# Transformer layers with convolution mixing, one core: a new order string for the mixing stage, three gate products tied behind a layer norm's mean, and a feed-forward whose down products run two blocks behind

## The chip, the cores and the metric

The kernel runs as one program on one core of a Trainium2 chip. The metric is the device time of one execution in microseconds (us). Names of engines: PE is the matrix engine (TensorE), DVE the vector engine, ACT the scalar engine, POOL the general engine (GpSimd), SP the engine that here only issues loads. A "product" below is one matmul instruction.

## The reference, cut to what matters

256 tokens of width 1024 pass through two layers (a gated delta rule layer and a sliding window attention layer, each followed by a gated feed-forward), and then through a third block: mixing (a convolution branch and an attention branch, joined by gates) and an expert layer. The parts that the change touches:

```python
def conv_gated_mlp(hn, w_up, conv_w, conv_b, w_down):      # twice, hidden width 2816
    u = causal_dwconv(hn @ w_up, conv_w, conv_b)           # 3 taps
    gate, val = jnp.split(u, 2, axis=-1)
    return (jax.nn.silu(gate) * val) @ w_down

def conformer_conv(a_in, dw_w, dw_b, ln_g, ln_b, w_pw):    # 1024 channels, 31 taps
    u = a_in[..., :CONV_DIM] * jax.nn.sigmoid(a_in[..., CONV_DIM:])
    u = lax.conv_general_dilated(u, dw_w[:, None, :], ...) + dw_b
    u = layernorm(u, ln_g, ln_b)
    u = jax.nn.silu(u)
    return u @ w_pw

# mixing, z = rmsnorm_2(x) @ w_in
gates = jax.nn.sigmoid(z[..., o_v:]).reshape(b, s, 2, d)
merged = gates[:, :, 0, :] * conv_out + gates[:, :, 1, :] * attn_out
x = x + merged @ w_out
```

## The kernel before

Activations lie transposed: 1024 features are 8 blocks of 128 partitions, and the 256 tokens are the free axis. Every float32 product is made of three products on split operands: `mm3` (L247 to L251) multiplies the weight's high part with the activation's high part (L249) and low part (L250), and the weight's low part with the activation's high part (L251). `wsplit` (L233 to L242) loads 512 KB of a weight (`raw`, issued by SP), rounds it on ACT (`wh`, L242) and subtracts on POOL or DVE (`wl`, L233); a table `LOW` for each stage says on which. `raw`, `wh` and `wl` have four buffers each, so weights run up to four pieces ahead. `proj` is one projection of 256 output columns: 2 weight pieces, 48 products. `kouter` adds 256 hidden features to four accumulators (`pa`): also 48 products.

The stages follow one another: delta rule layer (0 to some 290 us in the trace), feed-forward 0 (to 508), window attention (to 600), feed-forward 1 (to 800), mixing (to some 1075), expert layer (to the end).

**Feed-forward** (`ffn`). A loop over 11 blocks of 256 hidden features. A block makes two projections (gate and value), multiplies them with the norm's factor (L784), runs the three taps (ACT L789, DVE L791), Silu (ACT L794), the product of gate and value (DVE L795), and splits it into `gh` (ACT L798) and `gl` (DVE L799). `lower` then makes the block's down product with `kouter`; it is called for the block before the one just made (`pend`). `residual` adds the accumulators to the stream (DVE L292) and splits the result for the next stage (ACT L373, DVE L374).

**Mixing.** `play` walks through the string `MIX`; each item calls a function: `c0` to `c3` conv_in (two projections for 256 channels), `d0` to `d15` half the taps of one block of 128 channels (`conv`: the first tap on ACT at L1363, 30 multiply-adds on DVE at L1366, on an accumulator that alternates between two for even and odd blocks), `q`, `k`, `S`, `P`, `o` the attention, `g0` to `g7` a gate product (`gate`, L1382: one projection and one DVE multiplication), `L0` center, `N0` norm, `w` the pointwise product of the convolution branch, `e` the output product. `center` sums the convolution's channels with products against ones (`colsum`, L329), forms the mean (DVE L1399), spreads it over partitions (`rowcast`, L309) and subtracts it (DVE L1402). `norm` squares (ACT L315, L318), adds (DVE L319), sums again on PE (L329), takes the power -1/2 (DVE L338, POOL L339), spreads it (L309), multiplies (DVE L1415), applies Silu (ACT L1417) and splits into `upad` (ACT L1420) and `qT` (DVE L1421), the operands of `w0`.

The text order isn't the engines' order: the framework's scheduler reads the program, keeps data dependencies, and writes down a fixed order for each engine. `tc.issue_after(x)` makes it put what follows behind the instruction x. At run time each engine takes its own list strictly in order and waits where an operand is missing.

Of the kernel before, what the change touches and what calls it, by code (L numbers as in the profile page):

```python
# [11 lines left out]
F32R = mybir.dt.float32r  # L12
# [9 lines left out]
P = 128  # L22
T = 256
D = 1024
DB = D // P
# [5 lines left out]
C_SL = 320  # L31
# [7 lines left out]
def shape_constants():  # L39
# [7 lines left out]
    for k in range(DB):  # L47
# [24 lines left out]

GDN = "d0 d1 d2 z0 p0 d3 p1 p2 p3 b0 v1 v0 z1 i0 s1 v2 s0 z2 i2 o1 v3 o0 s2 z3 s3 o2 o3"
SWA = "q2 q0 S0 S1 P0 q1 S3 S2 P1 S4 P3 o0 P2 P4 q3 S5 o1 S7 P7 S6 P5 P6 o2 o3"
MIX = ("c0 q0 d0 d1 q1 d2 c1 d3 k0 d4 S0 S1 d5 P0 q2 d6 P1 S2 c2 d7 S3 P2 d8 q3 P3 d9 S4 c3 d10 S5 P4 d11 g4 S6 d12 "
       "P5 g5 S7 d13 P6 g6 d14 P7 g7 d15 s8 s12 o0 o1 o2 o3 a0 g0 g1 L0 g2 g3 N0 R0 s0 s4 w0 w1 e0 w2 e1 w3 e2 e3")
PEER = " ".join([f"q{i} k{i}" for i in range(8)] + [f"T{i}" for i in range(8)] + [f"u{i}" for i in range(32)])


# [18 lines left out]
class Net:  # L98
# [21 lines left out]
    def t(self, pool, shape, tag, dt=F32, **kw):  # L120
        return pool.tile(shape, dt, tag=tag, name=self.nm(tag), **kw)
# [184 lines left out]


    def rowcast(self, out, col):
        self.nc.tensor.matmul(out, col.to_broadcast([P, P]), self.ident, start=True, stop=True)  # L309

    def tokstat(self, src, pool, tag):

# [446 lines left out]
    def ffn(self, l, nxt, hook=None, each=None):  # L759
        nc, tc, I, t = self.nc, self.tc, self.I, self.t  # L760
        up, down = I["ffn_w_up"][l], I["ffn_w_down"][l]
        cw, cb = self.fconv[l], self.fbias[l]
        self.stage = "ffn"
        x = self.input(self.v["ffn_norm_w"][:, 8 * l : 8 * l + 8])
        with tc.tile_pool(name=f"ffn{l}", bufs=2) as fp:
            _, rrow = self.rstd(self.hT, fp, "sq")
            acc = None
            pend = []
            self.wide, self.nwide = True, NW[0]

            def lower(i, gh, gl):
                nonlocal acc
                if acc is None:
                    acc = self.acc4()
                self.kouter(acc, down, (2 * i, 2 * i + 1), [(gh[:, kk, :], gl[:, kk, :]) for kk in range(2)],
                            i == 0, i == 10)

            for i in range(11):
                if hook:
                    hook(i)  # L780
                cv = []
                for part in range(2):
                    ps = self.proj(up, part * 2816 + 256 * i, x)
                    nc.vector.tensor_mul(ps, ps, self.bc(rrow))  # L784
                    o = t(fp, [P, 2, T], f"cv{part}")
                    for m in range(2):
                        blk = part * 22 + 2 * i + m
                        w = [cw[j][:, blk : blk + 1] for j in range(3)]
                        nc.scalar.activation(o[:, m, :], ps[:, m, :], AF.Identity, scale=w[2], bias=cb[:, blk : blk + 1])  # L789
                        for d in range(1, 3):  # L790
                            nc.vector.scalar_tensor_tensor(o[:, m, d:], ps[:, m, : T - d], w[2 - d], o[:, m, d:],  # L791
                                                           op0=ALU.mult, op1=ALU.add)
                    cv.append(o)
                nc.scalar.activation(cv[0], cv[0], AF.Silu)  # L794
                nc.vector.tensor_mul(cv[0], cv[0], cv[1])  # L795
                gh = t(fp, [P, 2, T], "gh", F32R, bufs=3)
                gl = t(fp, [P, 2, T], "gl", F32R, bufs=3)
                nc.scalar.copy(gh, cv[0])  # L798
                nc.vector.tensor_sub(gl, cv[0], gh.bitcast(F32))  # L799
                pend.append((i, gh, gl))  # L800
                if len(pend) > 1:
                    lower(*pend.pop(0))
            lower(*pend.pop(0))
            self.residual(acc, nxt, None, each)


# [520 lines left out]
    def mix(self):  # L1327
        nc, tc, I, t = self.nc, self.tc, self.I, self.t
        w_in = I["w_in_2"][0]
        wf = self.v["final_norm_w"]  # L1330
        self.stage = "mix"
        x = self.input(self.wfg)
        with tc.tile_pool(name="mix", bufs=1, reuse_waits="tile") as mp, \
# [9 lines left out]
            rrow = self.rrow(rcol)  # L1343
# [10 lines left out]
            qT = t(mp, [P, DB, T], "qT")  # L1354
# [26 lines left out]
            def gate(i):  # L1381
                nc.vector.tensor_mul(gates[:, 2 * i : 2 * i + 2, :], self.proj(w_in, 3584 + 256 * i, x), self.bc(rrow))  # L1382

            def sig(i):
                nc.scalar.activation(gates[:, i : i + 4, :], gates[:, i : i + 4, :], AF.Sigmoid)

# [53 lines left out]
            def resnorm(_):  # L1440

                row = self.rrow(r1, ap, "sc256")
                for k in range(DB):
# [2 lines left out]

            self.wide, self.nwide = True, NW[3]
            self.play(MIX, c=conv_in, d=conv, k=lambda _: self.heads_kv(w_in, 3072, 3328, x, rrow, rcol, kT, v),
                      q=lambda i: self.heads_q(w_in, 2048, x, rrow, qT, i, self.c[:, C_SL : C_SL + DB]), g=gate, s=sig,
                      S=lambda u: self.scores(a, u), P=lambda u: self.values(a, u), o=lambda i: self.out_kv(a, i),  # L1450
                      a=attention, L=center, N=norm, w=point, e=out, R=resnorm)
            self.xq = ExitStack()
# [79 lines left out]
```

## Time and profile before

| | |
|---|---|
| median of 3 runs | 1987.35 us (1985.11 to 1990.6) |
| profiled execution, its own time | 1986.34 us |
| its span in the trace | 1984.6 us |
| mean granted TensorE clock | 0.973 |
| PE busy | 1848.3 us, 93% of the span |
| DVE busy | 1438.0 us, 72% |
| ACT busy | 956.5 us, 48% |
| POOL busy | 671.8 us, 34% |

The profiled execution is 1.0 us faster than the median; what is worked out from its trace is a difference, and is taken off the median too. "Busy" counts an instruction from start to end, and products on PE overlap: one lasts some 0.28 us at full clock, while a new one starts every 0.11 to 0.12 us.

### The profile page before, as it was taken

Reading aid. Unit: us, or ns where it says so; the run is one execution under the profiler, and the core shown is the slowest. Engines: PE = TensorE matmul, PEld = TensorE weight load, DVE = VectorE, ACT = ScalarE, POOL = GpSimd, SP = SyncE. Lnnn points to the kernel's source line nnn. Section 1 sums busy time; section 2 is a strip of 40 time slices with the busy share of each in tenths; the row PEclk is TensorE's granted clock in tenths of the full one; section 3 lists DMA queues with packets and bytes.
Section 4 is the critical chain, followed back from the end, with each engine's and each line's share of the span. In section 5 each row is a group of like instructions: output and inputs, shape, how many; then the busy total and the mean of one; then the engine's idle time right before and its main releaser. Section 6 shows DMA issues by size and latency. Waiting matters only on the chain. (4 is left out here: it accounts for less than half of the span.)

```text
span 1984.6 us, 36930 instructions
## 1 busy us (share of the span) xinstructions
PE 1848.3 (93%) x14537; PEld 1747.2 (88%) x14537; DVE 1438.0 (72%) x2765; ACT 956.5 (48%) x1419; POOL 671.8 (34%) x309
## 2 busy tenths in 40 slices
PE   7979999999899999999968978889999999999998
PEld 7879999999889999989968968779999988887886
DVE  6786656666546666588864799999888878875555
ACT  5744435555656555456444533433333443444443
POOL 4444333444323444655634423334333300000000
PEclk9989999999899999999979999999999999999999
DMA  6454236666424666443524555555555555555665
GB/s 198 118 160 139 86 107 201 191 192 193 134 86 128 212 192 185 135 139 108 170 86 139 161 128 149 140 137 160 155 161 154 149 170 160 163 159 169 195 195 171
DMA packets 243435, 306.29 MB, mean 154 GB/s; under 512 B 26076, under 2 KB 213821, under 8 KB 243133
## 3 DMA queue, kind: packets, MB, share of 16 engines
q1 hardware_dynamic: 240864, 302.84, 50.6%
q8 instruction: 114, 1.87, 0.4%
q10 hardware_dynamic: 2237, 1.07, 0.2%
q14 instruction: 60, 0.49, 0.1%
q0 software_dynamic: 160, 0.02, 0.0%
HBM read 298.60 MB, written 4.74 MB: 153 GB/s over the span
## 5 line engine op out<-in xcount | busy, mean ns | idle before, releaser
L233 POOL TENSOR_TENSOR wl<-raw,wh 128x1024 fp32r<-128x1024 f32 (+1 forms) x196 | 470.5, 2404 | 558.5 <-ACT wh L242 499.8
L242 ACT CAST wh<-raw 128x1024 fp32r<-128x1024 f32 (+1 forms) x285 | 297.8, 1047 | 319.2 <-issue 111.9
L233 DVE TENSOR_TENSOR wl<-raw,wh 128x1024 fp32r<-128x1024 f32 x233 | 294.4, 1264 | 162.2 <-ACT wh L1103 103.4
L251 PE MATMUL pp<-xh,wl 128*128 128x256 f32 x1392 | 394.5, 284 | 16.4 <-DVE wl L1009 16.3
L249 PE MATMUL pp<-xh,wh 128*128 128x256 f32 x1392 | 394.9, 284 | 15.1 <-DVE kq L491 10.3
L251 PE MATMUL pa<-xh,wl 128*128 128x256 f32 (+1 forms) x1336 | 382.0, 286 | 19.7 <-DVE wl L1009 19.6
L249 PE MATMUL pa<-xh,wh 128*128 128x256 f32 (+1 forms) x1336 | 382.9, 287 | 14.4 <-ACT hT L304 6.2
L250 PE MATMUL pp<-xl,wh 128*128 128x256 f32 x1392 | 393.1, 282 | 2.1 <-DVE xl L374 2.1
L250 PE MATMUL pa<-xl,wh 128*128 128x256 f32 (+1 forms) x1336 | 381.1, 285 | 2.0 <-DVE xl L374 1.9
L251 PEld LDWEIGHTS pp<-xh,wl 128*128 128x128 f32 x1392 | 267.0, 192 | 18.8 <-DVE wl L1009 18.3
L249 PEld LDWEIGHTS pp<-xh,wh 128*128 128x128 f32 x1392 | 267.1, 192 | 16.9 <-issue 10.7
L251 PEld LDWEIGHTS pa<-xh,wl 128*128 128x128 f32 (+1 forms) x1336 | 257.3, 193 | 22.4 <-DVE wl L1009 22.4
L249 PEld LDWEIGHTS pa<-xh,wh 128*128 128x128 f32 (+1 forms) x1336 | 257.3, 193 | 16.5 <-ACT hT L304 6.6
L250 PEld LDWEIGHTS pp<-xl,wh 128*128 128x128 f32 x1392 | 266.8, 192 | 2.5 <-DVE xl L374 2.3
L1009 POOL TENSOR_TENSOR wl<-rt,wh 128x1024 fp32r<-128x1024 f32 x64 | 166.0, 2594 | 291.1 <-ACT wh L994 209.2
L250 PEld LDWEIGHTS pa<-xl,wh 128*128 128x128 f32 (+1 forms) x1336 | 257.3, 193 | 3.2 <-DVE xl L374 2.4
L994 ACT CAST wh<-rt 128x1024 fp32r<-128x1024 f32 x128 | 134.3, 1049 | 240.6 <-PE pa L250 104.2
L1103 ACT CAST wh<-raw 128x1024 fp32r<-128x1024 f32 x128 | 135.0, 1055 | 216.4 <-PE pa L1113 210.1
L1112 PE MATMUL pa<-wl,rt 128*128 128x512 f32 x512 | 201.7, 394 | 0.0
L1113 PE MATMUL pa<-wh,rt 128*128 128x512 f32 x512 | 199.5, 391 | 0.0
L1111 PE MATMUL pa<-wh,rt 128*128 128x512 f32 x512 | 164.6, 394 | 1.4 <-ACT rt L1097 1.4
L1154 POOL TENSOR_TENSOR fsb<-fsb,mhalf 128x1 f32<-128x1 f32 x2 | 1.1, 550 | 393.8 <-DVE fsb L1153 393.8
(433 smaller groups left out, 3575.4 us busy)
## 6 DMA issues: line engine op xcount, KB each, us to landing
raw<-in_peer_u_dram SPq DMA_DIRECT2D x512, 128.0 KB
raw<-in_peer_v_dram SPq DMA_DIRECT2D x128, 512.0 KB
raw<-in_ffn_w_up_dram SPq DMA_DIRECT2D x88, 512.0 KB
raw<-in_a_w_in_dram SPq DMA_DIRECT2D x48, 512.0 KB
raw<-in_ffn_w_down_dram SPq DMA_DIRECT2D x44, 512.0 KB
raw<-in_w_in_dram SPq DMA_DIRECT2D x44, 512.0 KB
raw<-in_a_w_out_dram SPq DMA_DIRECT2D x16, 512.0 KB
raw<-in_peer_w_query_dram SPq DMA_DIRECT2D x16, 512.0 KB
```

What stands on the lines that cost most here:

```text
L233: (self.nc.vector if order[self.turn % len(order)] == "D" else self.nc.gpsimd).tensor_tensor(out, raw, high, op=ALU.subtract)
L242: nc.scalar.copy(wh, raw)
L249: mm(out, wh, xh, start=start, stop=False, skip_group_check=skip)
L250: mm(out, wh, xl, start=False, stop=False, skip_group_check=skip)
L251: mm(out, wl, xh, start=False, stop=stop, skip_group_check=skip)
L994: nc.scalar.copy(uh.rearrange("p f (b e) -> p f b e", b=4), rv)
L1009: eng.tensor_tensor(lo.rearrange("p f (b e) -> p f b e", b=4), rv, high.bitcast(F32).rearrange("p f (b e) -> p f b e", b=4), op=ALU.subtract)
L1103: nc.scalar.copy(vh, raw)
L1111: nc.tensor.matmul(o, w2[:, 0, i, s], vh[:, c], start=first, stop=False)
L1112: nc.tensor.matmul(o, w2[:, 0, i, s], vl[:, c], start=False, stop=False)
L1113: nc.tensor.matmul(o, w2[:, 1, i, s], vh[:, c], start=False, stop=last)
L1154: nc.gpsimd.tensor_tensor(o, o, self.mhalf(), op=ALU.pow)
```

## The change

The string MIX gets another order: the convolution's items stand earlier, `g4` to `g7` later. `g1`, `g2` and `g3` become `h1`, `h2` and `h3`, the same products by a function `late`, which puts them behind the last `rowcast` so far: `h1` and `h2` stand behind `L0` (the cast of the mean), `h3` behind `N0`. In the feed-forward `pend` holds two blocks instead of one, `gh` and `gl` get a fourth buffer, and the last two blocks' down products come after the loop.

```diff
-MIX = ("c0 q0 d0 d1 q1 d2 c1 d3 k0 d4 S0 S1 d5 P0 q2 d6 P1 S2 c2 d7 S3 P2 d8 q3 P3 d9 S4 c3 d10 S5 P4 d11 g4 S6 d12 "
-       "P5 g5 S7 d13 P6 g6 d14 P7 g7 d15 s8 s12 o0 o1 o2 o3 a0 g0 g1 L0 g2 g3 N0 R0 s0 s4 w0 w1 e0 w2 e1 w3 e2 e3")
+MIX = ("c0 q0 d0 q1 d1 k0 d2 c1 d3 S0 d4 S1 q2 d5 P0 d6 c2 S2 d7 P1 d8 S3 q3 d9 c3 d10 P2 S4 d11 P3 d12 S5 d13 "
+       "P4 S6 d14 P5 d15 S7 P6 g4 P7 g5 g6 g7 s8 s12 o0 o1 o2 o3 a0 g0 L0 h1 h2 N0 h3 R0 s0 s4 w0 w1 e0 w2 e1 w3 e2 e3")
...
     def rowcast(self, out, col):
-        self.nc.tensor.matmul(out, col.to_broadcast([P, P]), self.ident, start=True, stop=True)
+        self.cast = self.nc.tensor.matmul(out, col.to_broadcast([P, P]), self.ident, start=True, stop=True)
...
-                gh = t(fp, [P, 2, T], "gh", F32R, bufs=3)
-                gl = t(fp, [P, 2, T], "gl", F32R, bufs=3)
+                gh = t(fp, [P, 2, T], "gh", F32R, bufs=4)
+                gl = t(fp, [P, 2, T], "gl", F32R, bufs=4)
                 nc.scalar.copy(gh, cv[0])
                 nc.vector.tensor_sub(gl, cv[0], gh.bitcast(F32))
                 pend.append((i, gh, gl))
-                if len(pend) > 1:
+                if len(pend) > 2:
                     lower(*pend.pop(0))
-            lower(*pend.pop(0))
+            for p in pend:
+                lower(*p)
             self.residual(acc, nxt, None, each)
...
+            def late(i):
+
+                with tc.issue_after(self.cast.ins):
+                    gate(i)
...
-                      q=..., g=gate, s=sig,
+                      q=..., g=gate, h=late, s=sig,
```

What the engines' lists say now is shown at three places. The first is PE at the end of feed-forward 0; `pp` is the last up projection of block 10 (its operand `xh` is the stage's input), `pa` the accumulators, and the number behind `gh` and `gl` names the block's buffer. Before:

```order
L251 MATMUL pp_5697<-xh_3570,wl_5732 128x256
L249 MATMUL pa_3928<-gh_5564,wh_5774 128x256
...
L251 MATMUL pa_3931<-gh_5564,wl_5782 128x256
L249 MATMUL pa_3928<-gh_5768,wh_5834 128x256
L249 MATMUL pa_3929<-gh_5768,wh_5834 128x256
L249 MATMUL pa_3930<-gh_5768,wh_5834 128x256
```

And with the change, at the same place:

```order
L251 MATMUL pp_5637<-xh_3570,wl_5672 128x256
L249 MATMUL pa_4072<-gh_5299,wh_5714 128x256
...
L251 MATMUL pa_4075<-gh_5299,wl_5722 128x256
L249 MATMUL pa_4072<-gh_5504,wh_5774 128x256
...
L251 MATMUL pa_4075<-gh_5504,wl_5782 128x256
L249 MATMUL pa_4072<-gh_5708,wh_5834 128x256
L250 MATMUL pa_4072<-gl_5709,wh_5834 128x256
```

Behind the last up product there stood 48 products on the block before (`gh_5564`) and then those on the last block; now there stand 96 on two earlier blocks ahead of those on the last (`gh_5708`). Feed-forward 1 ends in the same way.

The second place is PE around the layer norm of the mixing stage; `conv` is the convolution's result, `mu` the mean, `sc` the sum of squares, `rcol` and `r` the two factors that are spread, `xh_9260` the mixing stage's input, which marks a gate product, and `upad`, `qT` the operands of `w0`. Before:

```order
L329 MATMUL pm_11498<-ones_85,conv_9332 128x1 x14
L249 MATMUL pa_11521<-xh_9260,wh_11524 128x256
...
L249 MATMUL pp_11583<-xh_9260,wh_11586 128x256
...
L329 MATMUL pm_11498<-ones_85,conv_9332 128x1 x2
L309 MATMUL pm_11516<-c_head_81,mu_11497 128x128 x2
L329 MATMUL pm_11656<-ones_85,sc_1537_11645 128x1 x4
L309 MATMUL pm_11664<-c_head_81,rcol_11661 128x128 x2
L309 MATMUL pm_11693<-c_head_81,r_1241_9314 128x128 x2
L249 MATMUL pp_11714<-upad_11667,wh_11717 128x256
```

With the change:

```order
L329 MATMUL pm_11436<-ones_85,conv_9332 128x1 x16
L309 MATMUL pm_11454<-c_head_81,mu_11435 128x128 x2
L249 MATMUL pa_11459<-xh_9260,wh_11462 128x256
...
L249 MATMUL pa_11521<-xh_9260,wh_11524 128x256
...
L329 MATMUL pm_11594<-ones_85,sc_1530_11583 128x1 x4
L309 MATMUL pm_11602<-c_head_81,rcol_11599 128x128 x2
L309 MATMUL pm_11693<-c_head_81,r_1241_9314 128x128 x2
L249 MATMUL pa_11631<-xh_9260,wh_11634 128x256
...
L249 MATMUL pp_11714<-upad_11605,wh_11717 128x256
```

The gate products `g1` to `g3` (48 products each) stood ahead of the mean's last sum; now `h1` and `h2` stand between the cast of the mean and the sum of squares (`sc`), and `h3` between the last cast and `w0`. `g0` stays ahead.

The third place is DVE's list from the last gate product before the mean on; `pm` at L1366 (L1367 with the change) is the convolution's accumulator. Before:

```order
L1382 TENSOR_TENSOR gates_9342<-pa_11521,rrow_9327 128x512
L1366 SCALAR_TENSOR_TENSOR pm_9333<-upad_9329,colsdw_48_207,pm_9333 128x256 x5
L233 TENSOR_TENSOR wl_11784<-raw_11780,wh_11782 128x1024
L1366 SCALAR_TENSOR_TENSOR pm_9333<-upad_9329,colsdw_48_207,pm_9333 128x256
L1382 TENSOR_TENSOR gates_9342<-pp_11583,rrow_9327 128x512
L1366 SCALAR_TENSOR_TENSOR pm_9333<-upad_9329,colsdw_48_207,pm_9333 128x256 x5
L1366 SCALAR_TENSOR_TENSOR conv_9332<-upad_9329,colsdw_48_207,pm_9333 128x256
L1399 TENSOR_SCALAR mu_11497<-pm_11498 128x2
```

With the change, through to the operands of `w0`:

```order
L1383 TENSOR_TENSOR gates_9342<-pp_11373,rrow_9327 128x512
L1367 SCALAR_TENSOR_TENSOR pm_9333<-upad_9329,colsdw_45_201,pm_9333 128x256 x15
L1367 SCALAR_TENSOR_TENSOR pm_9333<-upad_9329,colsdw_48_207,pm_9333 128x256 x14
L1367 SCALAR_TENSOR_TENSOR conv_9332<-upad_9329,colsdw_48_207,pm_9333 128x256
L1405 TENSOR_SCALAR mu_11435<-pm_11436 128x2
...
L1383 TENSOR_TENSOR gates_9342<-pa_11521,rrow_9327 128x512
L338 TENSOR_SCALAR rcol_11599<-pm_11594 128x2
...
L1427 TENSOR_TENSOR qT_11606<-pp_11607,upad_11605 128x512
L233 TENSOR_TENSOR wl_11784<-raw_11780,wh_11782 128x1024
L1383 TENSOR_TENSOR gates_9342<-pa_11631,rrow_9327 128x512
L1427 TENSOR_TENSOR qT_11606<-pa_11613,upad_11605 128x512
```

Three gate multiplications and two weight low parts have left the stretch ahead of the mean; the multiplications of `h1` and `h2` stand ahead of the norm's `rcol`, and that of `h3` between the first and the second quarter of `qT`. Over the whole stage, 98 of the 240 multiply-adds stood behind the last scores (S7, the last L1208) before, and 120 stand behind them now, while 108 fewer PE rows stand ahead of them.

## Rows read from the trace of the kernel before

**Rows 1.** The page: busy time, share of the span and instructions of each engine.

```profile
PE 1848.3 (93%) x14537; PEld 1747.2 (88%) x14537; DVE 1438.0 (72%) x2765; ACT 956.5 (48%) x1419; POOL 671.8 (34%) x309
```

**Rows 2.** Windows of feed-forward 0: length, busy time and count per engine, PEclk, DMA.

```profile
340.00:360.00 20.00, 20.00 (x174) 20.00 (x173) 14.29 (x19) 10.65 (x15) 8.98 (x4) 1.00 0.69 237
...
500.00:506.00 6.00, 5.71 (x26) 5.71 (x27) 1.54 (x4) 0.47 (x1) 0.00 (x0) 0.50 0.26 87
```

**Rows 3.** Timeline of PE, end of feed-forward 0: start, length, instruction [idle before, releaser].

```profile
490.34 0.28 PE L251 MATMUL pp<-xh,wl 128*128 128x256 f32 x1
...
498.18 0.74 PE L249 MATMUL pa<-gh,wh 128*128 128x256 f32 x4 [1.91 <-ACT gh L798]
500.29 0.58 PE L250 MATMUL pa<-gl,wh 128*128 128x256 f32 x1 [1.38 <-DVE gl L799]
...
508.18 0.28 PE L251 MATMUL pa<-gh,wl 128*128 128x256 f32 x1
```

**Rows 4.** Timelines of DVE, ACT and POOL at the same place.

```profile
498.16 2.08 DVE L799 TENSOR_TENSOR gl<-cv,gh 128x512 fp32r<-128x512 f32 x1 [0.69 <-ACT gh L798]
...
507.25 0.70 DVE L292 TENSOR_TENSOR pa<-pa,hT 128x512 f32<-128x512 f32 x1 [0.77 <-PE pa L251]
507.85 0.87 DVE L374 SCALAR_TENSOR_TENSOR xl<-pa,colsv,xh 128x256 fp32r<-128x256 f32 x2
...
497.51 0.62 ACT L798 CAST gh<-cv 128x512 fp32r<-128x512 f32 x1 [0.28 <-DVE cv L795]
...
497.31 2.38 POOL L233 TENSOR_TENSOR wl<-raw,wh 128x1024 fp32r<-128x1024 f32 x1 [0.38 <-ACT wh L242]
```

**Rows 5.** Line L799 from 330 to 480 us: durations in ns, minimum/median/maximum.

```profile
L799 DVE TENSOR_TENSOR gl<-cv,gh x9: 676/677/691, 339.1 to 465.5; 128x512 fp32r<-128x512 f32 x9
```

**Rows 6.** Timeline of PE, end of feed-forward 1.

```profile
782.63 0.28 PE L251 MATMUL pp<-xh,wl 128*128 128x256 f32 x1
...
790.49 0.74 PE L249 MATMUL pa<-gh,wh 128*128 128x256 f32 x4 [1.85 <-ACT gh L798]
792.64 0.38 PE L250 MATMUL pa<-gl,wh 128*128 128x256 f32 x1 [1.40 <-DVE gl L799]
...
799.38 0.28 PE L251 MATMUL pa<-gh,wl 128*128 128x256 f32 x1
```

**Rows 7.** Windows of the mixing stage: up to the last scores, to the mean, behind it.

```profile
820.00:934.50 114.50, 111.42 (x925) 106.45 (x924) 97.14 (x258) 67.53 (x127) 72.31 (x31) 0.99 0.45 142
934.50:1004.10 69.60, 64.47 (x538) 63.63 (x536) 59.61 (x118) 32.41 (x42) 40.98 (x17) 0.98 0.48 152
...
1006.00:1024.00 18.00, 6.74 (x28) 5.87 (x27) 13.05 (x23) 9.40 (x17) 0.69 (x1) 0.50 0.03 10
```

**Rows 8.** Timeline of DVE: a wait behind the last scores, and the convolution's end.

```profile
938.25 0.16 DVE L1219 TENSOR_TENSOR den<-den,es 128x4 f32<-128x4 f32 x1 [2.05 <-ACT es L1213]
...
998.67 1.23 DVE L233 TENSOR_TENSOR wl<-raw,wh 128x1024 fp32r<-128x1024 f32 x1 [0.55 <-ACT wh L242]
...
1000.38 0.69 DVE L1382 TENSOR_TENSOR gates<-pp,rrow 128x512 f32<-128x512 f32 x1
1000.99 2.58 DVE L1366 SCALAR_TENSOR_TENSOR pm<-upad,colsdw,pm 128x256 f32<-128x256 f32 x5
```

**Rows 9.** Timeline of PE around the mean and ahead of w0.

```profile
1004.14 0.61 PE L329 MATMUL pm<-ones,conv 128*128 128x1 f32 x4 [3.80 <-DVE conv L1366]
1005.00 1.23 PE L309 MATMUL pm<-c_head,mu 128*128 128x128 f32 x4 [0.25 <-DVE mu L1399]
1011.09 1.84 PE L329 MATMUL pm<-ones,sc 128*128 128x1 f32 x8 [4.87 <-DVE sc L319]
1013.96 1.22 PE L309 MATMUL pm<-c_head,rcol 128*128 128x128 f32 x4 [1.03 <-POOL rcol L339]
1014.97 1.06 PE L309 MATMUL pm<-c_head,r 128*128 128x128 f32 x4
...
1021.98 0.58 PE L250 MATMUL pp<-qT,wh 128*128 128x256 f32 x1 [2.38 <-DVE qT L1421]
```

More of the change, by code (lines that the diff above doesn't have):

```diff
@@ L1448, in mix @@
             self.play(MIX, c=conv_in, d=conv, k=lambda _: self.heads_kv(w_in, 3072, 3328, x, rrow, rcol, kT, v),
-                      q=lambda i: self.heads_q(w_in, 2048, x, rrow, qT, i, self.c[:, C_SL : C_SL + DB]), g=gate, s=sig,
+                      q=lambda i: self.heads_q(w_in, 2048, x, rrow, qT, i, self.c[:, C_SL : C_SL + DB]), g=gate, h=late, s=sig,
                       S=lambda u: self.scores(a, u), P=lambda u: self.values(a, u), o=lambda i: self.out_kv(a, i),
```

## The prediction

> **What bounds the kernel now.** I read the busy times first: PE is busy 93% of the span and no other engine comes near [rows 1]. So time can be won in two ways: PE gets less to do, or it waits less and runs less at the low clock. The change removes no product, so only the second is open, and I went through the windows of the stages that it touches for places where PE isn't full.
>
> In the middle of a feed-forward PE is busy 20.00 of 20 us and starts 174 to 176 products in that time, one every 0.114 us, at granted clock 1.00 [rows 2]; an order changed inside it can win nothing. The end is different. The timeline shows two waits on the last block: 1.91 us for `gh` and 1.38 us for `gl`, and then products at clock 0.50, half of the full 2.4 GHz: 26 recorded in 5.71 us [rows 2, 3]. Feed-forward 1 ends alike, with 1.85 and 1.40 us [rows 6].
>
> In the mixing stage PE is busy 111.4 of 114.5 us up to the last scores and 64.5 of 69.6 us from there to the mean [rows 7]. Then it stands nearly empty: 6.74 of 18 us, at clock 0.50. The timeline names the chain: the last sum waits 3.80 us for the convolution on DVE, the sum of squares 4.87 us for DVE, and the first whole step of `w0` begins at 1021.98 [rows 9]. Until the mean DVE's convolution sets the time; behind it a chain through DVE, ACT, POOL and PE does.
>
> **Feed-forward.** Before, 48 products lie between the last up product (490.34) and those of the last block. They cover 490.45 to 496.27 (498.18 less its wait of 1.91), 0.117 us apart. The last `gh` is ready at 498.13, the last `gl` at 500.24: 9.9 us behind the last up product [rows 3, 4]. With the change 96 products lie there, 96 x 0.117 = 11.2 us. As PE is full until then, the same products are only in another order: the last up product comes 5.6 us earlier, `gl` 5.6 us earlier too, and the last block's products start without a wait with 1.3 us to spare. The end then follows at full pace: 490.45 + 95 x 0.117 = 501.6 in place of 508.18, 6.6 us. The waits themselves are 3.3 of this; the rest is the clock (from 500.29 on some 44 products take 7.89 us where 44 x 0.117 are 5.1, so 2.8) and a few tenths around four products that started alone. For feed-forward 1: 782.74 + 95 x 0.117 = 793.9 in place of 799.38 [rows 6], 5.5 us, its clock part being 6.74 - 5.1 = 1.6.
>
> What is late next is `residual`: its last four accumulators now close 12 x 0.117 = 1.4 us apart, and DVE needs 0.70 + 0.87 = 1.57 us for each [rows 4], so up to 4 x 0.17 = 0.7 us comes back per feed-forward, and I take that. The stages behind it keep their own waits on this chain. At the start two blocks of up projections run with no down product between them; DVE has 14.29 of 20 us there in the steady mix [rows 2] and the work only changes places, so I take nothing (at most 1 us). The extra buffer costs no time. Sum: (6.6 - 0.7) + (5.5 - 0.7) = **-10.7 us**; if only the waits go and the clock part stays, -6.5.
>
> The margin of 1.3 us is thin for one reason: `gl` took 2.08 us at the end, and 0.68 in each of nine cases in the middle [rows 4, 5]. The long one ran beside a POOL subtraction from 497.31 to 499.69. The Trainium skill (GPSIMD Engine Reference, the table of specifications) says that GpSimd shares its SBUF interfaces with VectorE and that a VectorE instruction with two SBUF inputs can contend; `gl` is such a one, and the rows agree. By that rule the long case stays possible with the change; my 9.9 us already holds it. One more `wl` now stands ahead of `gl` on DVE; at 1.23 us [rows 8] it would use up the margin, not more.
>
> **Mixing up to the mean.** Call M the time at which the last sum for the mean can run, 1004.14 [rows 9]. Ahead of the last scores DVE has 22 multiply-adds and 2 gate multiplications less: a multiply-add takes 2.58 / 5 = 0.52 us in a row, a multiplication 0.69 [rows 8], together 12.7 us. PE has 108 rows less there, 12.3 us. But the attention's units 4 to 7 now follow one another on PE with no projections between them, and each runs scores, DVE, ACT, transposes, ACT, values, DVE: a wait such as 2.05 us on ACT [rows 8] can come back for each unit. I take 1 to 2 us for the whole, and have the last scores 11 us sooner. Behind them stand 120 multiply-adds in place of 98: +11.5 us; against that 1 gate multiplication and 2 low parts less (0.69 + 2 x 1.23 = 3.2), and a part of DVE's 10 idle us there (59.6 busy of 69.6 [rows 7]), some 2 to 3 us, because long rows of multiply-adds meet fewer waits. M moves by -11 + 11.5 - 3.2 - 2.5 = **-5 us**, between -10 and +4: the lower end if most of the idle time goes, the upper if each of four units waits 2 us and nothing of the idle time goes.
>
> So PE has lost 3 x 48 x 0.114 = 16.4 us of products ahead of the mean, while the mean comes only 5 us sooner. It waits some 12 us more there.
>
> **Mixing behind the mean.** Before, from M: cast of the mean to M + 2.1 (1006.23), sum of squares at M + 6.95, last cast finished at M + 11.9 (1016.03), `w0` running from M + 17.8 [rows 9], at the low clock first. With the change the sum of squares stands behind `h1` and `h2` on PE: M + 2.1 + 96 x 0.114 = M + 13.0, and the products start cold. For the price of a cold start the two feed-forward ends give 1.6 and 2.8 us; I take 1.5 to 2. So the sum runs at M + 14.7, 7.8 us later than DVE has it ready. From there to the last cast took 4.94 us; with a warm PE (the two casts and the sum took 1.22, 1.06 and 1.84 at half clock) some 3.7: M + 18.4. Then `h3`, 5.5 us or 7 if cold, to M + 24 or 25.5; its multiplication stands on DVE ahead of three quarters of `qT`, which `w0` needs after its first few products, so up to 1 us more. The other chain, from the cast of `rcol` to `w0`, took 1021.98 - 1013.96 = 8.0 us: M + 16.8 + 8.0 = M + 24.8. `w0` runs from M + 25, now warm, where before it ran from M + 17.8 and lost 1.5 to 2 us to the clock: **+6 us**, between +5 and +8. The loads, ACT casts and low parts of the three products move with them; four buffers let those of `h1` and `h2` arrive while PE waits.
>
> The low clock is the row's (0.50 over 18 us [rows 7]). The Trainium skill (Perfetto Trace Analysis, Matmul Optimizations) has a rule that speaks against this part: matmuls should run back to back, because the engine's power state follows its use. Splitting three products into a pair and a single one, each behind a gap, is what it warns of; by it `h3` starts cold as well and the sum is the +8 end, where full pace alone gives the +5 end. No row of this kernel shows a product inside such a gap.
>
> Mixing together: -5 + 6 = **+1 us**, between -5 and +10.
>
> **Sum.** -10.7 + 1 = -9.7 us: 1986.34 - 9.7 = 1976.6 for the profiled execution, which is 1.0 under the median, so **1977.6**.
>
> **Rivals.** (1) *The mixing stage gives back more.* The convolution isn't really sooner on DVE: more of it stands behind the last scores than before. If M doesn't move, mixing costs +6 to +7 and the net is -4: 1983.5. For it: PE's hole grows ahead of the mean. Against: three multiplications and two low parts do leave DVE. (2) *The convolution ends 10 us sooner*, as DVE is idle 17 us before and 10 us behind the last scores [rows 7]: mixing -4, net -15, 1973. Against: it needs an attention without waits. (3) *The feed-forward keeps half its waits*, because `gl` slips behind POOL and the extra low part by more than the margin: -5 there, net -4, 1983.5. (4) *Slower.* The dense attention stretch starves DVE: units 4 to 7 wait for ACT one after the other. The net passes +6 when M comes 11 us later than before (-10.7 + 6 + 11), that is when the four units lose 4 us each against the 2.05 us of the row and no idle time is won back: 1994. (5) *The change doesn't do what it says*: the ties hold nothing back, since `h1` to `h3` would stand there anyway. The lists exclude it for PE's order; for the convolution it is rival 1.
>
> **How the numbers follow.** Chances: my sum 0.50, rival 1 0.22, rival 2 0.13, rival 3 0.09, rival 4 0.06. The spread of my sum is mostly M's. About 0.3%, 6 us, is what a measurement of this kernel can tell from no change (its three runs lie 5.5 us apart): below 1981.4 is faster. Faster: 0.47 of the first, 0.12 of the third, a little of rivals 1 and 3 (0.08): 0.67. Slower: rival 4, 0.06. Same: 0.27. The range 1968 to 1986 leaves out rival 4 and the ends of rivals 1 and 2; the first case alone has 1973 to 1982.
>
> **What would show it.** Right: no wait on `gh` or `gl` at the ends of both feed-forwards, clock 1.00 there, and the next stages 6 and then 11 us earlier; in mixing a wait of some 15 us ahead of the mean's sum, that sum 15 to 16 us ahead of its old time, the sum of squares directly behind `h2` with no wait, and `w0` at 25 us behind the mean. Wrong: a wait on `gl` behind 96 products; the last scores less than 6 us sooner, relative to the stage's start; waits on ACT between units 4 to 7 above 8 us; or `w0` less than 20 us behind the mean, which would say that PE takes `h1` and `h2` in time that I counted as lost.

## The result and the profile after

The changed kernel runs in 1973.78 us, the median of 4 runs (1972.85 to 1977.59), beside 1988.97 for the kernel before, whose runs now are 4: ratio 0.9935, 95% interval 0.9919 to 0.9951. By the ratio that is 12.9 us less, where 9.7 were forecast; the two medians lie 15.2 us apart. The profiled execution took 1973.69 us; its span is 1971.9 in place of 1984.6, 12.7 less.

The waits of PE at the ends of the two feed-forwards, from 470 to 510 us and from 760 to 800 us:

```profile
PE pp L250 <- DVE xl L374: 1.7, 1, 1.7
PE pa L250 <- DVE wl L233: 0.8, 1, 0.8
...
PE pa L250 <- DVE xl L374: 0.9, 1, 0.9
PE pa L249 <- ACT xh L373: 0.2, 1, 0.2
```

The waits for `gh` and `gl` are gone; what is left belongs to the next stage's operands. The timelines of DVE and PE at the end of feed-forward 0, and the window that was at clock 0.50 before:

```profile
493.58 0.68 DVE L799 TENSOR_TENSOR gl<-cv,gh 128x512 fp32r<-128x512 f32 x1
...
498.40 0.70 DVE L292 TENSOR_TENSOR pa<-pa,hT 128x512 f32<-128x512 f32 x1 [4.14 <-PE pa L251]
502.64 0.70 DVE L292 TENSOR_TENSOR pa<-pa,hT 128x512 f32<-128x512 f32 x1 [0.33 <-PE pa L251]
```

```profile
485.48 0.28 PE L249 MATMUL pa<-gh,wh 128*128 128x256 f32 x1
...
502.33 0.28 PE L251 MATMUL pa<-gh,wl 128*128 128x256 f32 x1
```

```profile
500.00:506.00 6.00, 5.17 (x44) 4.91 (x42) 4.90 (x8) 5.71 (x11) 1.80 (x2) 1.00 0.34 112
```

The last down product starts at 502.33 in place of 508.18 [rows 3]; 144 products start from 485.48 to then, one every 0.118 us. The last `gl` is ready at 494.26, 2.5 us ahead of the 97th of them. The clock stays at 1.00 where it had fallen [rows 2].

Around the mean of the mixing stage PE's timeline reads:

```profile
985.50 1.01 PE L329 MATMUL pm<-ones,conv 128*128 128x1 f32 x4 [14.86 <-DVE conv L1367]
986.76 1.22 PE L309 MATMUL pm<-c_head,mu 128*128 128x128 f32 x4 [0.25 <-DVE mu L1405]
999.64 0.95 PE L329 MATMUL pm<-ones,sc 128*128 128x1 f32 x8
1001.62 0.71 PE L309 MATMUL pm<-c_head,rcol 128*128 128x128 f32 x4 [1.03 <-POOL rcol L339]
1002.16 0.61 PE L309 MATMUL pm<-c_head,r 128*128 128x128 f32 x4
1009.13 0.39 PE L249 MATMUL pp<-upad,wh 128*128 128x256 f32 x1 [0.89 <-DVE qT L1427]
...
1011.46 0.39 PE L250 MATMUL pp<-qT,wh 128*128 128x256 f32 x1 [1.24 <-DVE qT L1427]
```

Against [rows 9]: the wait ahead of the mean has grown from 3.80 to 14.86 us; the sum of squares runs 14.1 us behind the mean's sum in place of 6.95, with no wait of its own, since PE was busy with `h1` and `h2` all that time; and `w0` begins 23.6 us behind it, and stalls once more for `qT`, which DVE makes behind the multiplication of `h3`.

To compare stages I take four marks on DVE: the last residual sum of a feed-forward (L292), the mixing stage's first copy (L349), the end of the convolution (`conv` at L1366 or L1367), and the first product multiplied with its gate behind `w0` (L1430, L1436). The rows at L1374 and L1375 (the second multiplication) and the first multiply-adds behind them are used further below. Before, and with the change:

```profile
508.64 0.69 DVE L292 TENSOR_TENSOR pa<-pa,hT 128x512 f32<-128x512 f32 x1
...
799.77 0.69 DVE L292 TENSOR_TENSOR pa<-pa,hT 128x512 f32<-128x512 f32 x1
...
816.55 0.42 DVE L349 COPY rrow<-pm 128x256 f32<-128x256 f32 x1 [3.26 <-PE pm L309]
820.92 0.70 DVE L1374 TENSOR_TENSOR pp<-pp,rrow 128x512 f32<-128x512 f32 x1 [3.07 <-PE pp L251]
...
823.05 3.11 DVE L1366 SCALAR_TENSOR_TENSOR pm<-upad,colsdw,pm 128x256 f32<-128x256 f32 x6 [0.64 <-ACT pm L1363]
...
1003.60 0.48 DVE L1366 SCALAR_TENSOR_TENSOR conv<-upad,colsdw,pm 128x256 f32<-128x256 f32 x1
1029.38 0.70 DVE L1430 TENSOR_TENSOR pp<-pp,gates 128x512 f32<-128x512 f32 x1 [5.67 <-PE pp L251]
```

```profile
789.42 0.70 DVE L292 TENSOR_TENSOR pa<-pa,hT 128x512 f32<-128x512 f32 x1 [0.36 <-PE pa L251]
...
805.75 0.42 DVE L349 COPY rrow<-pm 128x256 f32<-128x256 f32 x1 [0.92 <-PE pm L309]
806.82 0.69 DVE L1375 TENSOR_TENSOR pp<-pp,rrow 128x512 f32<-128x512 f32 x1
...
810.51 2.59 DVE L1367 SCALAR_TENSOR_TENSOR pm<-upad,colsdw,pm 128x256 f32<-128x256 f32 x5 [0.64 <-ACT pm L1364]
...
984.96 0.48 DVE L1367 SCALAR_TENSOR_TENSOR conv<-upad,colsdw,pm 128x256 f32<-128x256 f32 x1
1016.68 0.70 DVE L1436 TENSOR_TENSOR pp<-pp,gates 128x512 f32<-128x512 f32 x1 [4.08 <-PE pp L251]
```

The start of mixing has moved by -10.8 us, its length to the last mark from 212.8 to 210.9: -1.9. From that mark to the stage's end it is 39.06 us in both, and the expert layer takes 916.1 and 916.2. So in this pair of profiles 10.8 of the 12.7 us come ahead of mixing, and 1.9 in it: 7.8 us up to the convolution's end (187.5 to 179.7) less 5.9 behind it (25.3 to 31.2).

### The profile page after: what moved, and what is told of

It is laid out like the page before. It is cut to its first block, busy times and chain, and to the rows that moved or that the text cites. A ratio compares the mean times of both kernels' runs of the same rounds, so it can differ in the third digit from the quotient of the medians.

```text
span 1971.9 us, 36937 instructions
## 1 busy us (share of the span) xinstructions
PE 1849.7 (94%) x14537; PEld 1749.3 (89%) x14537; DVE 1435.8 (73%) x2765; ACT 956.0 (48%) x1418; POOL 673.5 (34%) x309
## 3 DMA queue, kind: packets, MB, share of 16 engines
q10 hardware_dynamic: 2237, 1.07, 0.2%
## 4 chain that ended last, share of the span: by engine, by line
PE 40%; DVE 8%; DMA 2%; issue 1%; SPq 1%; POOL 0%; ACT 0%; DVEq 0%; POOLq 0%
PE pa L1112 6%; PE pa L1113 6%; PE pa L1114 6%; PE pa L249 4%; PE pa L251 4%; PE pa L250 4%; PE pm L1086 3%; PE pp L251 2%; PE pp L250 2%; PE pp L249 2%; DVE rt L992 2%; DMA raw<-in_peer_u_dram 2%; DVE wl L1010 1%; DVE pm L1367 1%; SPq L990 1%
## 5 line engine op out<-in xcount | busy, mean ns | idle before, releaser
L251 PE MATMUL pa<-xh,wl 128*128 128x256 f32 (+1 forms) x1368 | 391.0, 286 | 19.2 <-DVE wl L1010 19.2
L249 PE MATMUL pa<-xh,wh 128*128 128x256 f32 (+1 forms) x1368 | 391.9, 287 | 14.8 <-ACT hT L304 6.2
L233 DVE TENSOR_TENSOR wl<-raw,wh 128x1024 fp32r<-128x1024 f32 x233 | 289.2, 1242 | 154.4 <-ACT wh L1104 103.5
L249 PE MATMUL pp<-xh,wh 128*128 128x256 f32 x1360 | 386.9, 284 | 12.5 <-DVE kq L491 9.7
L251 PE MATMUL pp<-xh,wl 128*128 128x256 f32 x1360 | 386.5, 284 | 12.3 <-DVE wl L1010 12.3
L250 PE MATMUL pa<-xl,wh 128*128 128x256 f32 (+1 forms) x1368 | 389.9, 285 | 1.0 <-DVE xl L374 0.9
L250 PE MATMUL pp<-xl,wh 128*128 128x256 f32 x1360 | 384.9, 283 | 1.7 <-DVE xl L374 1.7
L251 PEld LDWEIGHTS pa<-xh,wl 128*128 128x128 f32 (+1 forms) x1368 | 263.1, 192 | 21.5 <-DVE wl L1010 21.4
L249 PEld LDWEIGHTS pa<-xh,wh 128*128 128x128 f32 (+1 forms) x1368 | 263.5, 193 | 17.9 <-ACT hT L304 6.6
L251 PEld LDWEIGHTS pp<-xh,wl 128*128 128x128 f32 x1360 | 262.1, 193 | 14.1 <-DVE wl L1010 13.6
L250 PEld LDWEIGHTS pa<-xl,wh 128*128 128x128 f32 (+1 forms) x1368 | 263.5, 193 | 2.4 <-DVE xl L374 1.6
L1104 ACT CAST wh<-raw 128x1024 fp32r<-128x1024 f32 x128 | 135.0, 1055 | 216.4 <-PE pa L1114 210.2
```

The source lines that it names most:

```text
L233: (self.nc.vector if order[self.turn % len(order)] == "D" else self.nc.gpsimd).tensor_tensor(out, raw, high, op=ALU.subtract)
L249: mm(out, wh, xh, start=start, stop=False, skip_group_check=skip)
L250: mm(out, wh, xl, start=False, stop=False, skip_group_check=skip)
L251: mm(out, wl, xh, start=False, stop=stop, skip_group_check=skip)
L1104: nc.scalar.copy(vh, raw)
```

## The experiments

Theory: the feed-forward part gives some 11 us, and mixing about nothing, its gain ahead of the mean being eaten behind it. Rivals: the gain of mixing lies in the ties, or in the string; the feed-forward gain is only its waits. A stage can vary by some us between executions of the same instructions (below), so the table has the marks beside the ratios with their intervals. Each ratio is to the kernel before as it ran beside that experiment. "to conv" is from L349 to the end of the convolution, "behind" from there to the last mark.

| run | ratio, 95% interval | to conv | behind | mixing |
|---|---|---|---|---|
| before | 1 | 187.5 | 25.3 | 212.8 |
| changed | 0.9935 (0.9919 to 0.9951) | 179.7 | 31.2 | 210.9 |
| e1 feed-forward alone | 0.9942 (0.9920 to 0.9964) | 182.3 | 26.3 | 208.6 |
| e2 mixing alone | 1.0027 (1.0012 to 1.0042) | 183.3 | 33.8 | 217.1 |
| e3 old string, ties | 0.9924 (0.9899 to 0.9949) | 178.7 | 31.7 | 210.4 |
| e4 one product early | 0.9917 (0.9895 to 0.9939) | 183.1 | 27.0 | 210.2 |
| e5 all early, new string | 0.9912 (0.9891 to 0.9933) | 181.4 | 25.5 | 206.9 |
| e6 changed, first tap on DVE | 0.9918 (0.9888 to 0.9947) | 177.0 | 31.3 | 208.3 |
| e7 e1, first tap on DVE | 0.9896 (0.9873 to 0.9919) | 180.4 | 25.4 | 205.7 |
| e8 three blocks back | 0.9944 (0.9922 to 0.9966) | 177.7 | 31.5 | 209.2 |
| e9 changed, sinks early | 0.9954 (0.9938 to 0.9969) | 180.2 | 31.7 | 212.0 |
| e10 e5, tap, sinks | 0.9910 (0.9891 to 0.9929) | 182.6 | 26.6 | 209.2 |
| e11 e7, sinks | 0.9874 (0.9849 to 0.9899) | 180.6 | 25.5 | 206.1 |

**e1, e2: the parts alone.** e1 takes only the hunk on `pend`, `gh` and `gl`; e2 takes all but that hunk.

> The feed-forward part alone (down products two blocks back, four buffers), the old mixing string and no ties. My theory (the two parts add; a feed-forward end gains its waits and the low clock behind them): the gain that the changed kernel shows at the start of its mixing stage, 10.3 to 10.8 us, and nothing else, ratio 0.9946 to the kernel before; the mixing stage as long as before (the mean's last sum 188 us behind the stage's first vector copy). Rival A (only the waits count, the clock's part is given back by the next stage): 6.5 us, 0.9967. Rival B (the feed-forward's new pace also shifts the mixing stage's timing): a mixing stage that differs by more than 2 us.

> The mixing part alone (new string and the three ties), the feed-forward as before. My theory: mixing gains about 2 us (the mean 7.8 us sooner in the stage, the stretch from the mean to the first gated product of w0 31.2 us in place of 25.2), ratio 0.999, hard to tell from no change. Rival A (the mixing part is worth 6 us or more by itself and the feed-forward part less): 0.997 or lower. Rival B (it costs by itself): above 1.001.

The feed-forward alone gives as much as the whole change (0.9942, 0.9935). Its one profile doesn't have the gain where I expected it: mixing begins 2.9 us sooner than before, not 10.3 to 10.8. Both feed-forwards are as short there as in the changed kernel (188.8 and 190.1 us beside 189.0 and 190.4), but with the same instructions window attention takes 100.1 us in place of 96.4, and the stretch from the last residual sum of feed-forward 1 to the first copy 21.2 in place of 16.3 (e9 to e11 below). Mixing alone is slower than before by 0.12 to 0.42%, which my theory didn't have (rival B of e2). In the stage it adds 4.3 us to a kernel without the feed-forward part (212.8 to 217.1) and 2.3 us to one with it (208.6 to 210.9). Rival B of e1 held too: the same mixing text is 4.2 us shorter with the new feed-forward. The second multiplication of the mixing stage stands 4.37 us behind the first copy in the kernel before (820.92), waiting 3.07 us for PE, and 1.07 us in the changed kernel and in all others with the feed-forward part. PE's list explains it: with the feed-forward part the scheduler puts most of `c0`'s second projection ahead of the casts that the copy waits for, 127 products recorded between the last residual sum and the copy in place of 97. The stretch to the copy isn't longer for them (16.8 us before, 16.3 in the changed kernel). Of the 3.3 us between 4.37 and 1.07, 1.7 reach the first multiply-add of the convolution (6.50 us behind the copy before, 4.76 with the feed-forward part), since DVE then waits 1.68 us for ACT. The rest of e1's 5.2 us up to the convolution's end lies behind that, where the engines' lists differ too; which instructions make it isn't shown. e12 below, with the old lists, has 187.5 and 25.3 us as the kernel before, to 0.1 us.

e2's stretch behind the mean is 2.6 us longer than the changed kernel's with the same instructions; 1.1 of this lie ahead of the sum of squares. PE's windows there, from the mean's sum on:

```profile
1002.90:1005.40 2.50, 2.25 (x10) 2.16 (x11) 0.16 (x1) 0.00 (x0) 0.00 (x0) 0.50 0.00 0
1005.40:1011.40 6.00, 6.00 (x37) 6.00 (x37) 4.43 (x5) 3.38 (x5) 0.22 (x1) 0.66 0.00 0
1011.40:1017.00 5.60, 5.60 (x52) 5.60 (x51) 1.92 (x2) 3.07 (x3) 2.56 (x2) 1.00 0.37 112
```

And the same windows of the changed kernel:

```profile
985.50:988.00 2.50, 2.25 (x9) 2.16 (x10) 0.16 (x1) 0.00 (x0) 0.00 (x0) 0.50 0.00 0
988.00:994.00 6.00, 6.00 (x47) 6.00 (x47) 4.43 (x5) 3.29 (x5) 1.19 (x1) 0.85 0.00 0
```

In the first 6 us of `h1`, 37 products are recorded at clock 0.66 against 47 at 0.85: behind a wait of 15 us in both (15.33 and 14.86) the clock came back at another moment. So part of what e2's profile adds is this; its ratio, over 12 runs, stands without it.

**e3, e4, e5: string, ties, and how many products lie where.** In the string of the changed kernel, and in e3 with the old string ahead of it:

```diff
-... a0 g0 L0 h1 h2 N0 h3 R0 ...
+... a0 g0 g1 L0 h2 N0 h3 R0 ...       (e4)
+... a0 g0 g1 g2 g3 L0 N0 R0 ...       (e5)
```

> The feed-forward part and the three ties, but the old order of the string ahead of them. My theory (the string brings the convolution's end forward, the ties alone only take three multiplications and two low parts off the vector engine): the mean 3 to 4 us sooner in the stage than before in place of 7.8, the stretch behind it 31 us as with the change, so mixing about 2.5 us longer than before and 1980, ratio 0.996. Rival (the ties are what wins, by moving products into the hole behind the mean, and the string does nothing): as the changed kernel or better, 0.9935.

> The changed kernel with one of the three products back ahead of the mean (order a0 g0 g1 L0 h2 N0 h3): one product uses the 14.9 us hole ahead of the mean, one lies between the cast of the mean and the sum of squares, one behind the last cast. My theory (the sum of squares is late because it is queued behind two products, 11.7 us, where the vector engine has it ready after 4.9): the mean 1 to 2 us later in the stage than with the change, the sum of squares 8.3 us behind the mean in place of 14.1, the first gated product of w0 at 25.5 to 26.5 us behind the mean in place of 31.2, net 3.5 to 4.5 us faster than the changed kernel, ratio 0.9915. Rival (the stretch behind the mean is bound by vector and scalar engine, so the place of the products doesn't matter): the time of the changed kernel within 1 us, 0.9935.

> The changed kernel with all three products ahead of the mean again (a0 g0 g1 g2 g3 L0 N0, no ties), the new string and the feed-forward kept. Theory 1, formed after the first four runs (the ties win about 3.7 us ahead of the mean, by taking three multiplications and two low parts off the vector engine, and cost 5 to 8 behind it; the string wins nothing): from the stage's first vector copy to the mean 183 us in place of 179.8, from the mean to the first gated product 25.2 to 26.3 in place of 31.2, together 208 to 209 in place of 210.9, as in the run with the feed-forward part alone (208.6). Rival (the new string wins by itself, its gain being hidden by the ties): 204 or less.

e3 went against my theory: with the old string and the ties the convolution ends at 178.7 us, as soon as with the new string (179.7), and the time is the same within the intervals. So the string brings nothing that can be seen. What the edits of mixing bring forward, the ties do (182.3 to 178.7 from e1 to e3, 3.6 us; three multiplications and two low parts had been put at 3.2, and DVE's busy time up to that mark falls by 4.0, from 157.8 to 153.8). They cost 5.4 us behind it (26.3 to 31.7). e4 moves both as expected in direction, but not in sum: the mean 3.4 us later (1 to 2 expected), the stretch behind it 4.2 us shorter, no gain that the runs can tell from the changed kernel. e5 has the stretch of before (25.5), the mean only 1.7 us later than with the ties, and a stage 4 us shorter than the changed kernel: 206.9, between my 208 to 209 and the rival's 204, so it decides neither. Its ratio is lower than the changed kernel's, but the intervals overlap.

**e6, e7: the first tap.** The waits of DVE in the changed kernel from 810 to 985 us, and one of them:

```profile
DVE pm L1367 <- ACT pm L1364: 8.1, 6, 2.7
```

```profile
943.33 0.48 DVE L1367 SCALAR_TENSOR_TENSOR conv<-upad,colsdw,pm 128x256 f32<-128x256 f32 x1
945.92 2.59 DVE L1367 SCALAR_TENSOR_TENSOR pm<-upad,colsdw,pm 128x256 f32<-128x256 f32 x5 [2.12 <-ACT pm L1364]
```

One block's last multiply-add is done, and the next block's first waits for ACT.

```diff
-                    nc.scalar.activation(o, up[:, m, 0:T], AF.Identity, scale=w[0],
-                                         bias=self.v["conv_dw_b_2"][:, m : m + 1])
+                    nc.vector.tensor_scalar(o, up[:, m, 0:T], w[0], self.v["conv_dw_b_2"][:, m : m + 1],
+                                            op0=ALU.mult, op1=ALU.add)
```

> The changed kernel with the convolution's first tap of each block on the vector engine (one tensor_scalar in place of the activation), so that the vector engine no longer waits 7.4 us for it. Theory 1 (the vector engine's convolution sets when the mean comes): eight instructions of about 0.5 us more, 7.4 us of waits less, the mean 3 to 4 us sooner in the stage (176 in place of 179.8), and the first gated product by the same amount. Rival (what waits for the scalar engine would wait for the matrix engine instead): the mean within 1 us of 179.8.

> The feed-forward part alone with the first tap on the vector engine, old string, no ties. Theory 1: waits of 4.1 us there against eight instructions of 0.5 us: no gain, mean within 1 us of 182.4, mixing 208 to 209. Rival (each wait on the scalar engine also delays what follows it): 3 us or more sooner.

The mean comes 2.7 us sooner in e6 and 1.9 us sooner in e7, and the stage is 2.7 and 2.9 us shorter. That the convolution on DVE sets the mean is the row of PE's wait, 14.86 us for `conv`; the size of the tap's gain is near the noise: the changed kernel, e8 and e9 have 179.7, 177.7 and 180.2 up to that mark without it, and e10 (below) with it comes 1.2 us later than e5. e6 reached less than 3 to 4 us, e7 more than nothing. On the whole time e7 is 0.46% below e1, some 9 us, of which the mixing stage has 2.9; the rest isn't accounted for.

**e8: three blocks back,** `len(pend) > 3` and five buffers.

> The changed kernel with down products three blocks back and five buffers. My theory (96 products, 11.2 us, already cover the 9.9 us from the last up product to the last low part): no wait at the two feed-forward ends as with two blocks, the same time within 1 us up to the residual, ratio 0.9935 as the changed kernel. Rival (part of the gain is that blocks have more room all along): 3 us or more faster.

Neither end has a wait on `gh` or `gl`, as with two blocks, and the ratio isn't lower. Two blocks are enough.

**e9 to e11: the sinks, and a better version.** Between the last residual sum of feed-forward 1 and the mixing stage's second multiplication, the profiles with the feed-forward part had 17.4, 19.6 or 22.3 us. The place where they differ, on DVE and POOL in the changed kernel:

```profile
792.40 0.17 DVE L1296 TENSOR_SCALAR sink<-sink 128x16 f32<-128x16 f32 x1 [1.48 <-DMA sink<-in_attn_sink_dram]
...
790.10 4.74 POOL L233 TENSOR_TENSOR wl<-raw,wh 128x1024 fp32r<-128x1024 f32 x2 [3.00 <-ACT wh L242]
```

and in e1, with PE's wait behind it:

```profile
795.50 2.30 DVE L1296 TENSOR_SCALAR sink<-sink 128x16 f32<-128x16 f32 x1 [1.59 <-DMA sink<-in_attn_sink_dram]
...
793.09 4.68 POOL L233 TENSOR_TENSOR wl<-raw,wh 128x1024 fp32r<-128x1024 f32 x2 [3.00 <-ACT wh L242]
...
798.25 0.58 PE L250 MATMUL pa<-xl,wh 128*128 128x256 f32 x1 [3.10 <-DVE xl L374]
```

A multiplication of 16 numbers per partition takes 0.17 us if it starts as the first of two POOL subtractions ends, and 2.30 if the second has begun: it ends at 797.80, POOL at 797.77. The eleven profiles with the sinks in this place hold 22 such multiplications, one at each attention's start: 17 began together with a POOL subtraction or while one ran, took 1.76 to 2.37 us, and ended 0.03 us behind its end; the other five began 0.02 to 0.12 us ahead of the next subtraction and took 0.17 or 0.18. Whether its load lands 0.1 us sooner or later decides, and PE's split operand behind it is 2.2 us late. e9 loads and negates both sinks ahead of their stages:

```diff
                 if hook:
                     hook(i)
+                if i == 4:
+                    self.sk = self.sinks(self.c0, I["attn_sink_2" if l else "b_sinks"], f"sink{l}")
```

> The changed kernel with the two attention sinks loaded and negated ahead of their stages, in place of at the start of the attention and mixing stages. Theory 2, from the profiles so far (this 128x16 multiplication takes 0.17 us when POOL is between two subtractions and 1.8 to 2.4 us when one runs, lasting until that one ends; the split behind it comes late, PE waits, and the clock falls): the time from the last residual sum of feed-forward 1 to the second multiplication of the mixing stage 17.4 us or less in the profile, where four of eight profiles of kernels with the feed-forward part had 17.4, one 19.6 and three 22.3; on the mean over runs 2 to 4 us faster than the changed kernel there, and up to 1.5 us at the start of the window attention. Rival (the spread at that place comes from the loads, not from the small multiplication): no difference, ratio 0.9935.

> The feed-forward part and the new string, without the ties (all three products ahead of the mean), first tap on the vector engine, sinks early. Theory 1: the mean comes at 180 us or a little earlier in the stage, since PE had only 1.1 us of wait left ahead of it in the run without ties; the stretch behind it 25.4: mixing 205 to 206, 5 us less than with the change; with the sinks 7 to 9 us faster than the changed kernel, ratio 0.989. Rival (the ties are needed to make use of an earlier convolution): mixing 208 or more.

> The same with the old string: the feed-forward part, first tap on the vector engine, sinks early. Theory 1 (the string is worth nothing): mixing within 1.5 us of the kernel with the new string, ratio 0.989. Rival (the new string is worth something once the products are ahead of the mean): 2 us or more slower than with the new string.

The stretch is 16.8 us in each of e9, e10 and e11, so the cause at that place is shown. At the start of window attention, where the sink's multiplication was held in all eleven profiles, that stage takes 91.7 to 94.9 us in these three and 95.2 or more in all others. On the whole time e9 missed: 2 to 4 us were expected, and it shows no gain over the changed kernel (0.9954 beside 0.9935, the intervals overlap); nor does e10 over e5 or e11 over e7 clear of the intervals. e10 missed too: mixing takes 209.2 us, not 205 to 206. e11's mixing stage is 3.1 us shorter than e10's, where the old string was to make no difference or cost 2 us. e11, with the old string and no ties, is faster than the changed kernel (0.9874, interval 0.9849 to 0.9899, which doesn't meet 0.9919 to 0.9951): the version with the lowest ratio has the feed-forward part and none of the mixing part.

**e12: POOL away from the last `gl`.** In the kernel before, the stage for `LOW` was set to "last" (always DVE) around the last down block's `kouter`.

> The kernel before with one difference: the low parts of the last down block's weights of each feed-forward are made on the vector engine, so that POOL runs nothing beside the last gl. Theory 2 (a vector instruction with its operands in SBUF waits until a POOL subtraction that has begun is over): gl takes 0.68 us in place of 2.08 and 2.11; the wait for gl on PE at the end of each feed-forward, 1.4 us, goes, though the wait for gh may be up to 1.3 us longer by the extra low part ahead of it. Rival (gl is slow there for another reason): gl still takes 2 us.

It doesn't do what it was made for. POOL still ran a subtraction there, for a weight of the next stage, and `gl` was as slow as before:

```profile
498.35 2.08 DVE L801 TENSOR_TENSOR gl<-cv,gh 128x512 fp32r<-128x512 f32 x1 [0.69 <-ACT gh L800]
...
497.50 2.38 POOL L233 TENSOR_TENSOR wl<-raw,wh 128x1024 fp32r<-128x1024 f32 x1 [0.38 <-ACT wh L242]
```

`gl` ends at 500.43, 0.55 us behind the end of POOL's at 499.88, as before (500.24 and 499.69 [rows 4]). What this run was to decide, the changed kernel's trace shows at the product of gate and value (L795), which reads two SBUF operands as `gl` does:

```profile
491.02 1.50 DVE L795 TENSOR_TENSOR cv<-cv,cv 128x512 f32<-128x512 f32 x1
...
489.56 2.41 POOL L233 TENSOR_TENSOR wl<-raw,wh 128x1024 fp32r<-128x1024 f32 x1 [3.13 <-ACT wh L242]
```

Twenty of its 22 cases begin beside a running POOL subtraction; they take 1.00 to 2.90 us, and each ends 0.55 us behind POOL's end. The two others take 0.68 and 0.69. And the last `gl` of feed-forward 0, the instruction that took 2.08 us before [rows 4], takes 0.68 at 493.58, where POOL runs nothing.

## Why the prediction was right, and where not

**Feed-forward: right in mechanism and size.** Forecast -5.9 and -4.8 us, measured at the last residual sums -6.0 and a further -4.35 (508.64 to 502.64, 799.77 to 789.42), -10.8 at mixing's start. The lengths of the two stages, each from the last residual sum ahead of it to its own, say it with less noise: 194.4 to 196.0 and 195.0 to 195.7 us in the three profiles without the feed-forward part (before, e2, e12), 187.7 to 190.3 and 188.8 to 191.1 in the eleven with it. The means differ by 6.1 and 5.2 us, more than the waits of 3.3 us each, so waits and clock part are both gained. (e1's ratio alone wouldn't tell this from its rival A, since e1's mixing stage is 4.2 us shorter too.) The margin was 2.5 us, not 1.3, because no POOL subtraction met `gl`. Rival 3 didn't happen.

**Up to the mean: the sum nearly right (-7.8 for -5), its terms not.** The last scores did come sooner, 15.3 us (11 forecast), and more multiply-adds did stand behind them, so that 7.5 us came back. But these two terms were of the string, and e3 shows the same mean without it. Of the -7.8, e1 has 5.2 without any edit of mixing, because the feed-forward part changes the engines' lists there; I had looked for changes of order in mixing only where the text of mixing changed. The ties give 3.6 from e1 to e3 and 1.7 from e5 to the changed kernel, for which I had 3.2. That long rows of multiply-adds "meet fewer waits" came out at half: behind the last scores DVE's idle time fell from 10.0 to 8.8 us, 1.2 for the 2.5 that I took. Ahead of them it fell from 19.7 to 14.8, where I had counted 1 to 2 us more.

**Behind the mean: right, +5.9 for +6.** The sum of squares waits for two products, and `w0` for `h3` and for `qT` behind its multiplication. The cold start of `h1` cost 0.7 us (11.7 us from the end of the casts at 987.98 to the sum at 999.64, for 96 products that take 10.9 at full pace), where I had 1.5 to 2; worked out alike, the other profiles with the ties give 0.8 to 2.0 (e2 1.8, e4 2.0), so the size of that term was fair and this profile at its low end. From the sum to the last cast I had 3.7 us "with a warm PE"; halving the three times named there takes 2.1 off 4.94 and gives 2.9, and 3.1 were measured (999.64 to 1002.77).

**The net of mixing.** Forecast +1, measured -1.9, and this step failed in its accounting: it came near only because two errors had opposite signs. The edits of mixing cost 2 to 4 us in the stage (e1 against the changed kernel, e2 against before; on the whole time only e2's cost is clear of the noise), towards rival 1, and the feed-forward part gave mixing some 4 us that I had put at nothing (212.8 to 208.6; from e2 to the changed kernel 6.2, but there 2.6 lie in the stretch behind the mean, where both run the same instructions). The chance of 0.22 for rival 1 was too low for the edits taken alone. The dense attention stretch (rival 4) cost nothing that shows. The range that I gave for mixing, -5 to +10, doesn't follow from its parts either: -10 to +4 and +5 to +8 make -5 to +12.

## What to carry to other kernels

Work that is moved into a hole doesn't pay when what ends the hole is queued behind it on the same engine: here 144 products moved from ahead of the mean to behind it, which left 15 us of idle time in the one place, and 96 of them put 7 us on the chain in the other. When a scheduler writes the order, an edit in one stage can reorder the next: compare the engines' lists beyond the text that changed, and test each part alone. Where a wait on the matrix engine is followed by a low clock, it can cost more than its length: 3.3 us of waits cost 5 to 6 at the ends of the feed-forwards.

## What the runs showed of the hardware

A vector instruction with its operands in SBUF (where all tiles lie but those that PE writes its sums to, which lie in PSUM) can be held until a POOL subtraction that runs beside it ends: 0.17 against 2.30 us for the same 128x16 multiplication, and 0.69 against 1.00 to 2.90 for the 128x512 product at L795, 20 times in the changed kernel. The Trainium skill (Perfetto Trace Analysis, Optimizing Scalar/DVE Operations) says that the two share an SBUF read port, which some vector instructions hold as an exclusive lock; the rows agree that the two exclude each other, and here it is the vector instruction that is locked out. Not every vector instruction is: 129 of the convolution's multiply-adds in the changed kernel, whose accumulator lies in PSUM, begin beside a running POOL subtraction, and all take 0.48 to 0.49 us as the others do.

The clock behind a wait isn't the same in each execution. From 580 to 600 us, at the seam of window attention and feed-forward 1, the granted clock was 0.91 in the changed kernel and 0.69 in e1, whose lists of instructions for both stages are the same. What sets it was not found. Window attention takes 96.4 and 100.1 us in these two, and the expert layer, with the same lists in the changed kernel and in e8, 916.2 and 912.0. Together with the sinks this makes stages vary by up to 5 us from one profile to the next, so a difference of 2 us between single profiles, of which several stand above, is shown only where a list of instructions explains it.
